# A decoder block on one core: three column blocks of w_in side by side over the chunks of x, and later side work

## The chip, the cores and the metric

The kernel runs as one program on 1 core of one Trainium2 chip. The engines are TensorE (PE, with PEld for the loading of its stationary operand), VectorE (DVE), ScalarE (ACT), GpSimd (POOL) and SyncE (SP). The metric is the device time of one execution in microseconds (us). Before the change it is 1447.08 us, the median of three runs (1445.6 to 1448.22).

## The reference

One block of a decoder for 256 tokens of width 2048, all in float32:

```python
h = rmsnorm(x, ln_mix_g)
u_s5, q, f, i, g, gate_s5, gate_hgrn = split(h @ w_in)           # w_in: 2048 x 9216
y_s5   = s5_branch(u_s5, ...) @ w_proj_s5        # diagonal complex scan over time, then a GLU
y_hgrn = hgrn2_branch(q, f, i, g, ...) @ w_proj_hgrn             # gated linear recurrence, 8 heads
x = x + (sigmoid(gate_s5) * y_s5 + sigmoid(gate_hgrn) * y_hgrn) @ w_out
x = x + conv_glu_ffn(rmsnorm(x, ln_ffn_g), w_up, conv_w, conv_b, w_down)   # d_ff = 5632
return rmsnorm(x, ln_final_g)
```

The S5 branch has 64 groups of 16 channels with 64 complex states each. The change touches how the first product, `h @ w_in`, begins, and when the S5 branch is computed beside it.

## The kernel before

**Weights as a stream of steps.** Every large product is cut into jobs of 256 or 512 columns, and each job into steps of one weight tile of [128, 1024] (512 KB). There are 480 steps, run in the order of the list `steps`; the first 144 are w_in, the next 8 the GLU of S5, then 16 of `w_proj_s5`, then `w_proj_hgrn` from step 168 on. For each step SP loads the tile (`load_step`, L247, four buffers `wr`), ACT casts its high part `wh` (L256) and DVE subtracts the low part `wl` (`split_step`, L252, three buffers of each), and PE forms three products: high by high, high by low, low by high. A feature-major job (`fm_job`, L271; u, q, f and the GLU) has 24 matmuls of 256 columns in a step, a token-major job (`tm_job`, L304) 12 of 512. Loads are issued 5 steps ahead (`LOAD_AHEAD`), splits 2 steps ahead (`LA`).

**x.** x comes in four chunks of 512 columns, two DMAs each (`load_x_chunk`, L388). `x_chunk` (L393) transposes a chunk on PE with the identity from the constant array `cf`, and ACT and DVE write its high and low parts to `hT`, with the gain `ln_mix_g` on columns (`g_mix`). The rows' norms come in after the products: `x_norm` (L427) squares x in eight DVE instructions, takes a root on ACT and a Newton step on DVE, and broadcasts the result over the partitions with matmuls of diagonal tiles `dg` into `R_x` (L358). `x_params` (L440) transposes the packed parameters to `colA`.

**The front's order before.** Jobs run one after the other, so step g of the first job needs chunk g of x. SP issues `cf`, `ln_mix_g`, then chunk and weight tile in turn. Chunks 1 to 3 are transposed in the middle of steps 0 to 2 (`st.between`, L284 and L1327), and `x_norm` and `x_params` are emitted behind step 2 (`NORM_AT`). A product's epilogue is emitted one step after its job's last step (`run_later`, L1274).

**Who sets the order.** The program's text gives priorities; the framework's scheduler then fixes, when the program is built, the order of each engine's queue, from its own model of times, and may move an instruction ahead of one that it takes to be waiting. On the chip each engine runs its queue strictly in that order. `issue_after` (in `behind_x`, L414) keeps an instruction behind a given one.

**Side work.** S5 (`side_s5`, L570) and then HGRN2 (`side_hgrn`, L866) are generators that are advanced between weight steps (`side_run`, L1290). Two counters add up estimated costs of DVE and PE (`_dve_cost`, `_pe_cost`, L76 and L84); a piece of side work is emitted as long as DVE's counter is not above PE's, at most two pieces of S5 or three of HGRN2 in a step, from step `S5_START` = 3 on. DVE's counter is never left more than 4 us behind. The GLU's steps need all of S5, and step 168 all of HGRN2: what is missing by then is emitted at once (`force`).

S5 works through eight chunks `ct` of 128 channels. For each, `tables` (L730) adds angles on POOL (L734), rounds them on ACT (L737) and takes sines; `b_place` and `b_trans` (L746, L756) transpose the input matrices, and POOL copies 24 blocks of 32 rows to other partitions (`move`, L754); `b_proj` (L771) multiplies them into the PSUM bank `bu`; DVE rotates, scans and rotates back; `output` (L782) multiplies the states into `ax`, and after chunks 3 and 7 a GELU and a split give the GLU's operand `z`. The four matrices of S5 are loaded from ACT's queue at its beginning (L574 to L577).

PSUM holds two `mm` banks for products, one `bu`, and two `ax` for transposes and small products.

Of the kernel before, what the change touches and what calls it, by code (L numbers as in the profile page):

```python
# [30 lines left out]
# columns of the constant array  # L31
# [5 lines left out]
def _constants():  # L37
# [12 lines left out]
    # within blocks of 32: per level, the columns in second halves of blocks of 2L; then the diagonal  # L50
# [6 lines left out]
# 1/(2 pi) in parts of twelve bits  # L57
# [37 lines left out]
class Metered:  # L95
    """An engine that adds up what its instructions are estimated to take."""
# [14 lines left out]
def kernel(  # L111
# [29 lines left out]
    NORM_AT = 2  # L141
# [25 lines left out]
    class Chunks:  # L167
        """[128, n, 256] kept in units of four."""
# [17 lines left out]
    S.dma_start(out=cf, in_=cst_f)  # L186
# [11 lines left out]
    S.dma_start(out=packG, in_=rows(ln_mix_g))  # L198
# [41 lines left out]
    def weight_step(src, mm, need=None, extra_load=None):  # L240
        st = Step()
        st.src, st.mm, st.need, st.extra_load = src, mm, need, extra_load
        st.after = st.between = None
# [60 lines left out]
    def tm_job(wap, c0, width, nkc, kper, xs, epi, need=None, extra_load=None, apart=False):  # L304
        """psum[t, n] for the columns from c0 on; xs(kc) gives the stationary pair."""
# [4 lines left out]
        for g in range(ng):  # L310
            def mm(st, g=g):
# [10 lines left out]
                # all of a row's products together in a last round of several tiles, else the low parts last  # L322
# [22 lines left out]
    def rstd_of(dst, ssum, n, scale, bias=None):  # L345
        """dst = 1/sqrt(ssum*scale + eps) for [128, n]; a Newton step after the square root."""
# [11 lines left out]
    def broadcast_rows(dst, r):  # L358
        """dst[p, j*128 + t] = r[t, j] on every partition."""
# [18 lines left out]
    def warm_up(n, rhs):  # L378
        # matmuls that nothing reads keep the tensor engine's clock up until the first products
# [3 lines left out]
    def table_up():  # L383
        # the square root's table comes in before x does
# [8 lines left out]
    def x_chunk(g, between=None):  # L393
        """Four chunks of x*g, transposed and in two parts; the rows' norms come in after the products."""
        for h in range(2):
            if h == 1 and between is not None:
                between()
# [5 lines left out]
            for a in range(2):  # L403
                kc = 4 * g + 2 * h + a
                A.activation(out=hT[:, kc, 0, :], in_=ax[:, a * T:(a + 1) * T], func=AF.Copy, scale=g_mix[:, kc:kc + 1])
# [5 lines left out]
        box["x"] = [getattr(i, "ins", i) for i in (last, lastp)]  # L411

    @contextmanager
    def behind_x():  # L414
        """What is emitted here is queued behind the last chunk of x."""
        with tc.issue_after(box["x"][0]), tc.issue_after(box["x"][1]):
            yield

    def x_first():
# [3 lines left out]
        x_chunk(0, lambda: split_step(steps[0]))  # L423
        with behind_x():
            warm_up(WARM_H, ones)

    def x_norm():  # L427
        ss = cst.tile([P, 2, 4], F32, name="ss_x")
        for g in range(4):
# [961 lines left out]
```

## Time and profile before

| | |
|---|---|
| median of 3 runs | 1447.08 us (1445.6 to 1448.22) |
| the profiled execution's own time (its span) | 1446.9 us |
| busy: PE, PEld | 1408.5 us (97%), 1209.1 us (84%) |
| busy: DVE, ACT, POOL | 1065.1 us (74%), 749.1 us (52%), 205.6 us (14%) |
| mean granted TensorE clock | 0.989 |
| HBM read, written | 266.73 MB, 10.49 MB |

A timeline row gives start, duration, engine, line, operation, output<-inputs and count; in brackets stands the idle time of that engine before it and what ended it. L106 is the helper through which all PE and DVE instructions are recorded, so these are told apart by their tiles. A row of the waits gives who waited for whom, the total in us, the number of waits and the longest. A row of a stretch gives the busy time of PE, PEld, DVE, ACT and POOL, with the number of instructions in brackets, then the granted clock, the DMA share and GB/s. Busy time of PE is that of overlapping, pipelined matmuls; idle time of PE is what can be gained.

### The profile page before, as it was taken

To read this page: it belongs to the slowest core of one execution; us is meant where nothing else is said; L and a number is where in the kernel's file an instruction comes from. 1 tells how busy PE (TensorE), PEld (TensorE's weight loads), DVE (VectorE), ACT (ScalarE), POOL (GpSimd) and SP (SyncE) were. 2 spreads that over 40 slices of the span, in tenths; PEclk is the share of its full clock that TensorE was granted. 3 is DMA by queue.
4 is the path that set the end of the run, shared out by engine and by line. 5 is a ranking of instruction groups with operands and counts; after the bars stand their busy time and mean duration, and the time that the engine had idled before them with its cause. 6 is when DMAs were issued, how large, how long until landed. Compare 5 with 4: busy or idle time off the path is not lost.

```text
span 1446.9 us, 21528 instructions
## 1 busy us (share of the span) xinstructions
PE 1408.5 (97%) x8328; PEld 1209.1 (84%) x8328; DVE 1065.1 (74%) x1435; ACT 749.1 (52%) x944; POOL 205.6 (14%) x230
## 2 busy tenths in 40 slices
PE   9997989899999999999999999999999999999997
PEld 8996887786778988888888888888888888888886
DVE  6978988999996967755677777777777775545454
ACT  5353466565554465445555555555555554434343
POOL 3037416743560100000000000000000000000000
PEclk9999999999999999999999999999999999999999
DMA  7763746565667656766666666666666665666563
GB/s 242 197 210 118 207 154 217 178 181 167 214 184 220 218 175 223 220 213 212 198 188 189 189 189 189 189 189 190 189 189 189 188 188 192 195 198 201 192 194 128
DMA packets 215942, 278.62 MB, mean 193 GB/s; under 512 B 19937, under 2 KB 141041, under 8 KB 215840
## 3 DMA queue, kind: packets, MB, share of 16 engines
q1 hardware_dynamic: 198496, 266.57, 59.6%
q10 hardware_dynamic: 17088, 10.49, 2.3%
q8 instruction: 65, 1.06, 0.3%
q14 instruction: 37, 0.30, 0.1%
q0 software_dynamic: 256, 0.19, 0.0%
HBM read 266.73 MB, written 10.49 MB: 192 GB/s over the span
## 4 chain that ended last, share of the span: by engine, by line
PE 82%; DVE 4%; POOL 3%; issue 1%; ACT 0%; DVEq 0%; ACTq 0%
PE mm L106 74%; PE ax L106 7%; POOL u L754 3%; DVE u L106 3%; DVE wl L106 1%; PE bu L106 0%; ACT wh L256 0%; POOL u L734 0%; ACT u L1262 0%; DVE zmat L106 0%; DVE x2g L106 0%; DVE t L106 0%; ACT t L260 0%; ACT t L1246 0%; DVE fin L106 0%
## 5 line engine op out<-in xcount | busy, mean ns | idle before, releaser
L106 DVE TENSOR_TENSOR wl<-wr,wh 128x1024 fp32r<-128x1024 f32 x480 | 596.4, 1246 | 323.8 <-ACT wh L256 321.6
L256 ACT CAST wh<-wr 128x1024 fp32r<-128x1024 f32 x480 | 502.8, 1051 | 607.3 <-PE mm L106 433.6
L106 PE MATMUL mm<-x2g,wh 128*128 128x512 f32 x1408 | 352.6, 392 | 0.0
L106 PEld LDWEIGHTS mm<-x2g,wh 128*128 128x128 f32 x1408 | 253.3, 189 | 45.3
L106 PE MATMUL mm<-wh,u 128*128 128x512 f32 x1040 | 259.7, 391 | 0.0
L106 PEld LDWEIGHTS mm<-wh,u 128*128 128x128 f32 x1040 | 194.1, 188 | 39.7
L106 PEld LDWEIGHTS mm<-x2g,wl 128*128 128x128 f32 x1408 | 192.0, 190 | 13.6
L106 PE MATMUL mm<-wh,hT 128*128 128x512 f32 x768 | 196.6, 399 | 4.9 <-ACT wh L256 4.9
L106 PE MATMUL mm<-x2g,wl 128*128 128x256 f32 x1408 | 196.4, 282 | 0.0
L754 POOL TENSOR_SCALAR u<-t 32x256 fp32r<-32x256 f32 x192 | 167.5, 874 | 163.1 <-ACT t L260 151.4
L106 PEld LDWEIGHTS mm<-wh,hT 128*128 128x128 f32 x768 | 145.5, 192 | 38.5 <-ACT wh L256 5.4
L106 PE MATMUL mm<-wl,u 128*128 128x512 f32 x520 | 140.6, 390 | 0.0
L106 DVE TENSOR_TENSOR u<-u,u 128x512 f32<-128x512 f32 (+3 forms) x134 | 114.0, 874 | 0.3
L106 PEld LDWEIGHTS mm<-wl,u 128*128 128x128 f32 x520 | 97.4, 188 | 19.9
L106 PE MATMUL mm<-wl,hT 128*128 128x512 f32 x384 | 106.0, 397 | 6.6 <-DVE wl L106 6.6
L106 PE MATMUL mm<-hT,wh 128*128 128x256 f32 x768 | 105.1, 289 | 4.4 <-ACT wh L256 4.4
L106 PEld LDWEIGHTS mm<-hT,wh 128*128 128x128 f32 x768 | 98.5, 196 | 5.6 <-ACT wh L256 4.6
L106 PEld LDWEIGHTS mm<-wl,hT 128*128 128x128 f32 x384 | 72.7, 191 | 24.9 <-DVE wl L106 9.5
L106 DVE SCALAR_TENSOR_TENSOR t<-ub,colC,t 128x256 f32<-128x256 f32 x176 | 73.3, 478 | 0.0
L106 PE MATMUL mm<-hT,wl 128*128 128x256 f32 x384 | 55.1, 286 | 0.0
L106 PEld LDWEIGHTS mm<-hT,wl 128*128 128x128 f32 x384 | 50.3, 195 | 0.2 <-DVE wl L106 0.2
L106 DVE TENSOR_TENSOR_SCAN u<-mag,u 128x256 f32<-128x256 f32 x64 | 47.9, 800 | 0.1
(191 smaller groups left out, 894.3 us busy)
## 6 DMA issues: line engine op xcount, KB each, us to landing
wr<-in_w_up_dram SPq DMA_DIRECT2D x176, 512.0 KB, 4.5
wr<-in_w_in_dram SPq DMA_DIRECT2D x144, 512.0 KB, 4.3
wr<-in_w_down_dram SPq DMA_DIRECT2D x88, 512.0 KB, 4.7
wr<-in_w_out_dram SPq DMA_DIRECT2D x32, 512.0 KB, 4.1
wr<-in_w_proj_s_dram SPq DMA_DIRECT2D x16, 512.0 KB, 4.1
wr<-in_w_proj_hgrn_dram SPq DMA_DIRECT2D x16, 512.0 KB, 4.9
d<-t ACTq DMA_DIRECT2D x28, 256.0 KB, 4.4
rl<-d SPq DMA_DIRECT2D x16, 256.0 KB, 3.8
```

Of the source, the lines that this page charges most:

```text
L106: return fn(*args, **kw)
L256: A.copy(st.wh, st.w)
L754: G.tensor_scalar(out=dst, in0=src.bitcast(F32), scalar1=1.0, scalar2=0.0, op0=ALU.mult, op1=ALU.add)
```

## The change

- The first three jobs of w_in run side by side (`FRONT = 3`): the first 12 steps are reordered, so that chunk g of x serves three steps. SP's loads follow: a chunk of x, then three weight tiles. The third job's sums lie in the bank `bu`.
- These 12 steps, and what goes with them, are in a fixed order on SP, PE, ACT and DVE (`manual_schedule`), with splits one step ahead. Chunks 1 to 3 are transposed ahead of steps 2, 5 and 8, not in the middle of a step.
- The squares of a chunk follow its transposition (`x_squares`), and the rest of the norm and `x_params` stand behind step 9 (`NORM_AT = 3 * FRONT`).
- `cf` and `ln_mix_g` are loaded from ACT's queue; the four parameter loads go behind w10 on SP, and HGRN2's masks behind the weight of step 12.
- The planner's counters begin at zero at step 12, and S5's side work begins there. `behind_x` also holds ACT's instructions.

The removed comments are left out of the diff.

```diff
-    NORM_AT = 2
+    FRONT = 3
+    NORM_AT = 3 * FRONT
...
-    S.dma_start(out=cf, in_=cst_f)
+    A.dma_start(out=cf, in_=cst_f)
...
-    S.dma_start(out=packG, in_=rows(ln_mix_g))
+    A.dma_start(out=packG, in_=rows(ln_mix_g))
...
-        S.dma_start(out=v3(st.w, st.src.shape[1]), in_=st.src)
+        st.dma = S.dma_start(out=v3(st.w, st.src.shape[1]), in_=st.src)
...
-    def fm_job(wap, c0, nkc, xs, epi, need=None, extra_load=None, wide=False):
+    def fm_job(wap, c0, nkc, xs, epi, need=None, extra_load=None, wide=False, bank=mm_bank):
...
-                    box["ps"] = mm_bank()
+                    box["ps"] = bank()
...
-                    if part == 1 and st.between is not None:
-                        st.between()
...
-    def x_chunk(g, between=None):
+    def x_chunk(g):
...
-        box["x"] = [getattr(i, "ins", i) for i in (last, lastp)]
+        box["x"] = [getattr(i, "ins", i) for i in (last, lastp, lasta)]
...
-        x_chunk(0, lambda: split_step(steps[0]))
-        with behind_x():
-            warm_up(WARM_H, ones)
+        x_chunk(0)
+        warm_up(WARM_H, ones)
+        split_step(steps[0])
+        x_squares(0)
+
+    ss_x = cst.tile([P, 2, 4], F32, name="ss_x")
+
+    def x_squares(g):
+        for j in range(2):
+            xc = x_tok[j][g // 2][:, (g % 2) * 512:(g % 2) * 512 + 512]
+            junk = tmp()
+            V.scalar_tensor_tensor(out=junk, in0=xc, scalar=1.0, in1=xc, op0=ALU.mult, op1=ALU.mult,
+                                   accum_out=ss_x[:, j, g:g + 1])
...
-    u_jobs = [fm_job(w_in, 256 * p, 16, xs_h, epi_u(p)) for p in range(4)]
+    def front_bank():
+        uid[0] += 1
+        return psb.tile([P, 2, 512], F32, tag="bu", name=f"mf{uid[0]}")
+
+
+    u_jobs = [fm_job(w_in, 256 * p, 16, xs_h, epi_u(p), bank=front_bank if p == 2 else mm_bank) for p in range(4)]
+    steps[:4 * FRONT] = [steps[4 * p + g] for g in range(4) for p in range(FRONT)]
...
-        S.dma_start(out=mraw[:, 0:112], in_=cst_m)
-        V.tensor_copy(masks, v3(mraw[:, 0:80], 5))
+        with behind_x(), tc.issue_after(getattr(steps[4 * FRONT].dma, "ins", steps[4 * FRONT].dma)):
+            S.dma_start(out=mraw[:, 0:112], in_=cst_m)
+            V.tensor_copy(masks, v3(mraw[:, 0:80], 5))
...
+    def load_front(i):
+        if i % FRONT == 0 and i < 4 * FRONT:
+            load_x_chunk(i // FRONT)
+        load_step(steps[i])
+        if i == 3 * FRONT + 1:
+            with tc.issue_after(getattr(steps[i].dma, "ins", steps[i].dma)):
+                load_params()
...
+    with tc.manual_schedule(engines={ET.SP, ET.PE, ET.Activation, ET.DVE}):
+        for i in range(LOAD_AHEAD):
+            load_front(i)
+        table_up()
+        warm_up(WARM, ones)
+        x_first()
+        for i in range(4 * FRONT):
+            g, r = divmod(i, FRONT)
+            load_front(i + LOAD_AHEAD)
+            if r == FRONT - 1 and g < 3:
+                x_chunk(g + 1)
+            split_step(steps[i + 1])
+            if r == FRONT - 1 and g < 3:
+                x_squares(g + 1)
+            work(i, steps[i])
+            if i == NORM_AT:
+                x_norm()
+                x_params()
+    for i in range(1, LA):
+        split_step(steps[4 * FRONT + i])
+    load["dve"] = load["pe"] = 0.0
+    for i, st in enumerate(steps):
+        if i < 4 * FRONT:
+            continue
...
-        if i >= S5_START:
-            pauses[0] = 0
-            if i == S5_START:
-                with behind_x():
-                    side_run()
-            else:
+        pauses[0] = 0
+        if i == 4 * FRONT:
+            with behind_x():
                 side_run()
+        else:
+            side_run()
```

`work(i, st)` is the old loop's body from `run_later(i=i)` to the entry of the epilogue, without the norm.

More of the change, by code (lines that the diff above doesn't have):

```diff
@@ L242, in weight_step @@
         st.src, st.mm, st.need, st.extra_load = src, mm, need, extra_load
-        st.after = st.between = None
+        st.after = None
         steps.append(st)
@@ L391, in load_x_chunk @@
                         in_=x[0, j * P:(j + 1) * P, g * 512:(g + 1) * 512])
-    def x_chunk(g, between=None):
+    def x_chunk(g):
         for h in range(2):
-            if h == 1 and between is not None:
-                between()
             ax = axbank()
@@ L404, in x_chunk @@
                 kc = 4 * g + 2 * h + a
-                A.activation(out=hT[:, kc, 0, :], in_=ax[:, a * T:(a + 1) * T], func=AF.Copy, scale=g_mix[:, kc:kc + 1])
+                lasta = A.activation(out=hT[:, kc, 0, :], in_=ax[:, a * T:(a + 1) * T], func=AF.Copy,
+                                     scale=g_mix[:, kc:kc + 1])
             for a in range(2):
@@ L410, in x_chunk @@
                                               op0=ALU.mult, op1=ALU.subtract)
-        box["x"] = [getattr(i, "ins", i) for i in (last, lastp)]
+        box["x"] = [getattr(i, "ins", i) for i in (last, lastp, lasta)]
     @contextmanager
     def behind_x():
-        with tc.issue_after(box["x"][0]), tc.issue_after(box["x"][1]):
+        with tc.issue_after(box["x"][0]), tc.issue_after(box["x"][1]), tc.issue_after(box["x"][2]):
             yield
@@ L422, in x_first @@
         V.tensor_copy(g_mix, ax[:, 0:16])
-        x_chunk(0, lambda: split_step(steps[0]))
-        with behind_x():
-            warm_up(WARM_H, ones)
-    def x_norm():
-        ss = cst.tile([P, 2, 4], F32, name="ss_x")
-        for g in range(4):
-            for j in range(2):
-                xc = x_tok[j][g // 2][:, (g % 2) * 512:(g % 2) * 512 + 512]
-                junk = tmp()
-                V.scalar_tensor_tensor(out=junk, in0=xc, scalar=1.0, in1=xc, op0=ALU.mult, op1=ALU.mult,
-                                       accum_out=ss[:, j, g:g + 1])
+        x_chunk(0)
[9 more added lines that the diff above has]
+                                   accum_out=ss_x[:, j, g:g + 1])
+    def x_norm():
+        ss = ss_x
         ssum = cst.tile([P, 2], F32, name="ssum_x")
@@ L1284, in run_later @@
                 later.sort(key=lambda e: (e[0], e[1]))
-    S5_START = 3
     PAUSES = {"s5": 2, "hgrn": 3}
@@ L1313, in side_run, with work @@
                     return
-    for i in range(LOAD_AHEAD):
-        if i < 4:
-            load_x_chunk(i)
+    def load_front(i):
+        if i % FRONT == 0 and i < 4 * FRONT:
+            load_x_chunk(i // FRONT)
         load_step(steps[i])
-        if i == 4:
-            load_params()
-    table_up()
-    warm_up(WARM, ones)
-    x_first()
-    for i in range(1, LA):
-        split_step(steps[i])
-    for i in range(3):
-        steps[i].between = lambda i=i: x_chunk(i + 1)
-    load["dve"] = load["pe"] = 0.0
-    for i, st in enumerate(steps):
-        if i + LOAD_AHEAD < len(steps):
-            load_step(steps[i + LOAD_AHEAD])
-        if i + LA < len(steps):
-            split_step(steps[i + LA])
+        if i == 3 * FRONT + 1:
+            with tc.issue_after(getattr(steps[i].dma, "ins", steps[i].dma)):
+                load_params()
+    def work(i, st):
         run_later(i=i)
@@ L1344 @@
         st.mm(st)
-        if i == NORM_AT:
-            with behind_x():
-                x_norm()
-                x_params()
         if st.after is not None:
@@ L1351 @@
             later.append((i + 1, job, fn))
-        load["dve"] = max(load["dve"], load["pe"] - 4.0)
-        if i >= S5_START:
-            pauses[0] = 0
-            if i == S5_START:
-                with behind_x():
-                    side_run()
-            else:
+    ET = mybir.EngineType
+    with tc.manual_schedule(engines={ET.SP, ET.PE, ET.Activation, ET.DVE}):
[22 more added lines that the diff above has]
+            continue
+        if i + LOAD_AHEAD < len(steps):
+            load_front(i + LOAD_AHEAD)
+        if i + LA < len(steps):
+            split_step(steps[i + LA])
+        work(i, st)
+        load["dve"] = max(load["dve"], load["pe"] - 4.0)
+        pauses[0] = 0
+        if i == 4 * FRONT:
+            with behind_x():
                 side_run()
+        else:
+            side_run()
     run_later(i=len(steps) + 10)
```

## The prediction

> **What bounds the kernel now.** I read the page first, then stretches of 20 us, the waits of the tensor engine, and the timeline of the first 50 us and of the places where it waits. Columns of a timeline row: start, duration, engine, line, operation, out<-in, count, and in brackets the idle time before it with what ended it.
>
> ```profile
> span 1446.9 us, 21528 instructions
> PE 1408.5 (97%) x8328; PEld 1209.1 (84%) x8328; DVE 1065.1 (74%) x1435; ACT 749.1 (52%) x944; POOL 205.6 (14%) x230
> ...
> 120.00:140.00 20.00, 13.75 (x59) 9.99 (x57) 19.06 (x19) 3.56 (x4) 17.26 (x21) 1.00 0.36 105
> ...
> PE mm L106 <- ACT wh L256: 9.3, 2, 4.9
> ```
>
> PE is busy for 1408.5 of 1446.9 us, so 38 us at most is there to win, and most of it is not in the front: the worst stretch is 120 to 140 us, where PE has 13.75 us of work while DVE has 19.06 and POOL 17.26. The two waits for `wh` (9.3 us together, the longer 4.9) belong to S5's side work. No matmul is added or dropped by the change, so I cost waits and starts, against this execution's 1446.9 us. The median of the runs, 1447.08, is 0.2 above it.
>
> **The change part by part.** First the front, with the rows from which each step has its duration:
>
> ```profile
> 0.74 0.38 SPq L186 DMA_DIRECT2D cf<-in_cst_f_dram  x1
> 1.65 0.88 SPq L390 DMA_DIRECT2D u<-in_x_dram  x2
> 5.71 0.33 PE L106 MATMUL ax<-cf,u 128*128 128x128 f32 x1 [1.19 <-DMA u<-in_x_dram]
> 8.79 1.06 ACT L256 CAST wh<-wr 128x1024 fp32r<-128x1024 f32 x1
> 9.91 2.73 PE L106 MATMUL mm<-hT,wh 128*128 128x256 f32 x16
> 20.56 0.81 PE L106 MATMUL ax<-cf,u 128*128 128x128 f32 x6
> 20.97 1.57 ACT L405 ACTIVATE hT<-ax,g_mix 128x256 fp32r<-128x256 f32 x4 [0.73 <-PE ax L106]
> 21.84 1.66 DVE L106 SCALAR_TENSOR_TENSOR hT<-ax,g_mix,hT 128x256 fp32r<-128x256 f32 x4 [0.16 <-ACT hT L405]
> 23.42 0.68 DVE L106 SCALAR_TENSOR_TENSOR t<-u 128x512 f32<-128x512 f32 x1
> 29.45 0.15 DVE L106 TENSOR_REDUCE ssum_x<-ss_x 128x2 f32<-128x8 f32 x1
> 29.52 1.22 DVE L106 TENSOR_TENSOR wl<-wr,wh 128x1024 fp32r<-128x1024 f32 x1
> 29.64 0.29 ACT L350 ACTIVATE rss<-ssum_x,epsd 128x2 f32<-128x2 f32 x1 [1.36 <-DVE ssum_x L106]
> 33.13 0.16 DVE L106 TENSOR_TENSOR rss<-rss,rsv 128x2 f32<-128x2 f32 x1
> 33.72 0.48 DVE L106 TENSOR_SCALAR dg<-cf,r_x 128x128 f32<-128x128 f32 x2
> 37.47 0.27 PE L106 MATMUL ax<-cf,u 64*128 64x64 f32 x1 [1.30 <-DVE R_x L106]
> 47.10 1.12 PE L106 MATMUL mm<-hT,wl 128*128 128x256 f32 x8
> 48.06 2.08 PE L106 MATMUL mm<-hT,wh 128*128 128x256 f32 x16
> 49.98 1.12 PE L106 MATMUL mm<-hT,wl 128*128 128x256 f32 x8
> ...
> 461.09 1.07 PE L106 MATMUL mm<-wl,hT 128*128 128x512 f32 x4
> 463.81 1.07 PE L106 MATMUL mm<-wl,hT 128*128 128x512 f32 x4
> ```
>
> (a) *Constants to the second queue.* `cf` and `ln_mix_g` stand before x on SP, so x is issued at 1.65; in the new kernel x has SP's place at 0.74. The first x reaches PE at 5.71 after a wait for its DMA, and from there transposes, four evictions on ACT and the first CAST (8.79) lead to the first product at 9.91. All of it moves up by 1.65 − 0.74: **−0.9 us**. Bounds −0.9 and 0. ACT now issues the two small loads, 0.4 us each, ahead of its table load, and idles until its first eviction at 7.35 anyway.
>
> (b) *Squares spread.* The eight squares stand in one block on DVE, from 23.4 us to the split (1.22) ahead of the reduction at 29.45, so to 28.2, 0.6 apart. Splits of weights queue behind them, their buffers come free late, loads and CASTs slip, and the copy of `R_x` stands behind a late `wl`. PE, whose transpose at 37.47 needs that bank, waits 1.3 us. Spread over the chunks, this goes: **−1.3 us** (bounds −1.3 and 0).
>
> (c) *Norm in fixed order.* But the broadcast of the norm now stands on PE's queue right behind step 9, and step 10 behind it. Count from the end of the last chunk's transposes, which precede step 8. In the old rows these end at 21.37 (20.56 + 0.81), ACT's evictions start at −0.40 and end at +1.17, DVE's low parts end at +2.13 (21.84 + 1.66 − 21.37). In the new order ACT then casts `wh9` (1.06, to 2.1), DVE subtracts `wl9` (1.22, to 3.4), does two squares (to 4.6), `wl10` (to 5.8), and the reduction. Behind that, uncrowded, come ACT's root (0.19 later, 0.29 long) and six small DVE operations, 0.15 to 0.2 apart (four lie from 33.13 to 33.72), with the last one's 0.28: about 1.9 us from reduction to broadcast, so 7.6. PE has only steps 8 and 9 in between, each 2.88 (49.98 − 47.10): it runs dry at 5.8. **+1.8 us**, bounds 0 (if the squares are done earlier) and 3.5 (with the clock, below). Behind the waiting broadcast stand step 10 and all later products; DVE's `R_x` and `colA` copies, `wl11` and the first epilogue follow within 3 us, and `wl11` is wanted 5 us later, so nothing else is late.
>
> The half clock has its own rows (window, busy times of PE, PEld, DVE, ACT, POOL, granted clock, DMA):
>
> ```profile
> 4.33:7.74 3.41, 1.81 (x13) 1.34 (x13) 0.46 (x2) 0.39 (x2) 3.29 (x9) 1.00 1.00 314
> 7.74:11.16 3.42, 3.42 (x19) 3.33 (x18) 2.93 (x5) 2.11 (x5) 3.42 (x4) 0.50 1.06 389
> ```
>
> A stretch in which PE had 1.81 us of work in 3.41 was followed by one at clock 0.50. A wait of 1.8 us leaves 1.6 if it falls into one such stretch, which for an unknown phase is (3.41 − 1.8)/3.41 = 0.47 likely; its price is at most 3.41/2 = 1.7 us. I take 0. The Trainium skill (TensorE: Matmul & The Clock Gate, "What's actually happening") says that the clock drops after a whole idle window of about 3.4 us; by that there would be no such loss, while the row above shows a drop after a window that was half busy, so the bound stays.
>
> (d) *Other loads and the order of products.* Twelve steps take 12 × 2.88 us in either order; the 24 transposes (0.135 each) only stand before the products instead of among them. SP issues w1 and w2 before the second chunk of x, and x's third and fourth chunks behind loads that wait for a buffer; each chunk is wanted three steps (8.6 us) after the last, and even the first x, with the queue cold, was there 4.1 us after its issue (1.65 to 5.71), so nothing waits. The four parameter loads (0.4 us of SP each) go behind w10 and the mask load behind w12; their readers come at step 9 and in HGRN2. The third job's bank is S5's, first needed 20 steps later. All nothing. But S5's four matrix loads now follow step 12 on ACT's queue:
>
> ```profile
> 35.27 4.38 ACTq L575 DMA_DIRECT2D u<-in_s_b_im_dram  x1
> ...
> 43.93 2.95 ACT L256 CAST wh<-wr 128x1024 fp32r<-128x1024 f32 x3 [8.11 <-DVE u L106]
> ```
>
> For 8.1 us, to 43.93, ACT casts nothing and issues. Three split weights ahead are 3 × 2.88 = 8.6 us of cover, against 8.1 us of it and a CAST of 1.06: **+0.6 us** (bounds 0, as before, and 1.5).
>
> (e) *S5's loop of eight chunks.* Emission of side work follows a planner: per step PE gains 24 × 0.109 = 2.616 and DVE 0.065 + 0.00112 × 1.04 × 1024 = 1.258, and side work fills the 1.358 between. Adding up the code's own cost functions, S5 is 193.4 of DVE and 19.0 of PE. Before, DVE's lead from the squares lets it begin at step 6; now the counters begin at step 12 with zero. Replaying the two counters, `b_trans` of chunks 0, 1, 2 comes at steps 27, 29, 44 before and 33, 35, 49 after; the tables of chunks 1 and 2 at 37 and 50 before, 42 and 57 after. What hangs on that distance:
>
> ```profile
> 99.64 36.62 POOL L754 TENSOR_SCALAR u<-t 32x256 fp32r<-32x256 f32 x48 [22.38 <-ACT t L260]
> 136.35 2.17 POOL L734 TENSOR_TENSOR u<-u 128x1024 f32<-128x1024 f32 x1
> ...
> 138.55 1.15 ACT L737 ACTIVATE u<-u,roundc 128x1024 f32<-128x1024 f32 x1 [14.24 <-POOL u L734]
> 140.69 3.65 PE L106 MATMUL mm<-wh,hT 128*128 128x512 f32 x8 [4.92 <-ACT wh L256]
> ...
> 162.17 19.93 POOL L754 TENSOR_SCALAR u<-t 32x256 fp32r<-32x256 f32 x24 [23.66 <-ACT t L260]
> 182.18 3.80 POOL L734 TENSOR_TENSOR u<-u 128x1024 f32<-128x1024 f32 x2
> ...
> 186.27 3.78 PE L106 MATMUL mm<-hT,wh 128*128 128x256 f32 x16 [4.39 <-ACT wh L256]
> ```
>
> POOL copies 48 blocks (36.6 us), then adds the table; ACT's rounding waits for it at the head of its queue, the CASTs wait behind it, and PE runs out of weights. For chunk 1 the distance shrinks from 10 steps to 9, and four of them become steps of 2.72 us (463.81 − 461.09): PE runs dry 2.88 + 4 × 0.16 = 3.5 us earlier, and one more half-clock stretch (1.7) follows: +5.2. For chunk 2 it grows from 6 steps to 8, which covers the 4.39 us and the half clock behind it (16 products in 3.78 us there against 2.08 at full clock, and 0.9 more on the rest): −7.0. Sum **−1.8 us**, bounds −7.0 and +5.2. For chunks 3 to 7 I count no difference.
>
> (f) *S5's end.* By the same counters S5 ended at step 140; now it would end at 145, and step 144, the first of the GLU, forces the rest out just before it. Its chain:
>
> ```profile
> 464.81 1.07 PE L106 MATMUL ax<-u,u 128*32 128x256 f32 x16
> ...
> 466.75 1.06 ACT L797 ACTIVATE u<-u 128x1024 f32<-128x1024 f32 x1 [0.38 <-DVE u L106]
> ...
> 468.98 1.05 ACT L260 CAST u<-u 128x1024 fp32r<-128x1024 f32 x1
> ...
> 470.25 1.22 DVE L106 TENSOR_TENSOR u<-u,u 128x1024 fp32r<-128x1024 f32 x1
> ```
>
> From the end of the output products (465.88) to the low part (471.47) are 5.6 us, which five steps hid. Now step 144 alone (first half of z, 2.88) lies over them; a weight's CAST in the middle (0.9) can go behind: 5.6 − 2.9 − 0.8 = **+1.9 us**, bounds 0 and 5.
>
> (g) *HGRN2* is emitted at steps 145 to 166 instead of 141 to 161, and step 168 needs it. It ran to 557.04 (row below), two steps behind its emission; now it would end as step 168 starts: **+0.5 us**, bounds 0 and 4.
>
> ```profile
> 556.58 0.46 ACT L1031 ACTIVATE u<-ax,colA 128x256 fp32r<-128x256 f32 x1
> ```
>
> Sum: −0.9 − 1.3 + 1.8 + 0.6 − 1.8 + 1.9 + 0.5 = +0.8; 1446.9 + 0.8 + 0.2 = **1447.9 us**. The front gives back its gain, and S5's shift gives and takes.
>
> **Rivals.** *The first POOL wait does not grow* (the scheduler puts the rounding behind one more CAST, or the table's addition ahead of the copies, as no table after chunk 2's made PE wait for `wh`: two such waits in all). Then 1447.9 − 5.2 = 1442.7. Against it: both early tables did make it wait.
>
> *Short distances come back* (the other side). In the replay chunks 5, 6 and 7 have six steps between `b_trans` and the next table, where they had seven; the one distance of six before is chunk 2's, and it cost 7.0. It decides if POOL's 24 copies outlast those six steps, 6 × 2.72 = 16.3 us, and ACT already stands at the rounding; chunk 2's took 19.93. Once is 1447.9 + 7.0 = 1454.9. For it: the copies are slower where DVE is full. The Trainium skill (SBUF — State Buffer, "Who interferes with whom") says that GpSimd's reads are blocked for a whole DVE instruction with two SBUF inputs; 36.62/48 = 0.76 and 19.93/24 = 0.83 us a copy here agree with a length that varies. Against it: chunks 3 to 7 made no CAST wait.
>
> *The side work is late at both ends*: (f) and (g) at their bounds, 1447.9 + 3.1 + 3.5 = 1454.5, if DVE too is behind at step 144. Against it: that last stretch had DVE idle.
>
> *The change does not shorten the front at all*: x's landing unmoved, (a) = 0, with (c) as costed: 1448.8, inside the forecast's band; so is (c) hidden, 1446.1.
>
> **How the numbers follow.** A measurement of this kernel tells about 0.2%, 2.9 us, from no change, so "same" is 1444.2 to 1450.0. Forecast 0.36; first wait does not grow 0.33 (faster); short distances 0.21 and late side work 0.10 (slower, 0.31). The likeliest case's own range is 1444 to 1450. For 8 in 10: down to 1440.5 (the faster case and another 2.2, (a) to (d) at their better ends), up to 1456 (the slower cases and 1.1 more).
>
> **What would show it.** (a) x's first issue at 0.7 and the first product near 9.0. (b), (c): no wait for `R_x`, but a wait of PE for `dg` of 1 to 2.5 us at 41 to 45 us. (d) A wait for `wh` under 1.5 us near 60 us. (e) One wait for `wh` of 7 to 9 us near 150 us, and none near 190. (f) A wait for `u` before step 145, near 482 us. It is wrong if the loop's waits of PE for `wh`, `wl` and `bu` differ in sum by over 5 us, or if the front ends over 2 us earlier than before.

## The result, and the profile after

The changed kernel takes **1459.53 us** (median of 4 runs, 1457.74 to 1460.66) against 1446.86 us before (4 runs, 1445.6 to 1448.22): ratio **1.0081**, 95% interval 1.0066 to 1.0095. It is slower by 12.7 us; the forecast was 1447.9, the range ended at 1456.0. The profiled execution is the quickest of the four: 1457.74 us for a span of 1455.7, so some 2 us of a time lie outside the span. The spans differ by 8.8 us.

The page after, its span and busy times:

```profile
span 1455.7 us, 21517 instructions
...
PE 1404.8 (97%) x8328; PEld 1204.1 (83%) x8328; DVE 1062.3 (73%) x1435; ACT 750.2 (52%) x946; POOL 193.2 (13%) x230
```

PE is busy for 3.7 us less than before, and still the span is longer: what was added is waiting. PE's waits after (who waited for whom: us in total, times, longest):

```profile
PE mm L106 <- ACT wh L257: 16.1, 6, 7.7
PE bu L106 <- POOL u L762: 13.5, 6, 6.5
PE mm L106 <- DVE wl L106: 6.1, 5, 2.7
PE ax L106 <- DVE dg L106: 2.1, 2, 1.9
PE ax L106 <- DMA u<-in_ln_mix_g_dram: 1.4, 1, 1.4
```

The wait for `R_x` is gone. Waits for `wh` grew from 9.3 to 16.1 us, and those of `bu` for POOL's copies from 7.0 (longest 2.5) to 13.5 (longest 6.5). To place the loss I took from both timelines the end of every step's low-part products (`mm<-…wl`) and subtracted:

| steps | terms of the prediction | foreseen, us | difference gained in the trace, us | sum so far |
|---|---|---|---|---|
| 0 to 11 | (a), (b), (c) | −0.4 | −1.3 | −1.3 |
| 12 to 15 | (d) | +0.6 | +1.9 | +0.7 |
| 16 to 63 | (e), chunks 1 and 2 | −1.8 | −2.1 | −1.4 |
| 64 to 143 | (e), chunks 3 to 7 | 0 | **+7.0** | +5.6 |
| 144 to 175 | (f), (g) | +2.4 | +3.2 | +8.8 |

From step 175 to the end the difference stays at 8.8 us. So most of the loss is where the prediction counted "no difference". Its own sign of being wrong is there too: PE's waits for `wh`, `wl` and `bu` add up to 35.7 us, against 24.6 before, and a difference of 5 was its limit. First the front, in the timeline after:

```profile
5.69 1.35 PE L106 MATMUL ax<-cf,u 16*128 16x16 f32 x9 [1.44 <-DMA u<-in_ln_mix_g_dram]
...
9.19 2.05 PE L106 MATMUL mm<-hT,wh 128*128 128x256 f32 x15 [0.81 <-ACT wh L257]
...
43.26 0.68 PE L106 MATMUL ax<-dg,ones 128*128 128x128 f32 x4 [1.94 <-DVE dg L106]
...
52.65 0.72 PE L106 MATMUL ax<-cf,u 64*128 64x64 f32 x4
...
59.05 2.94 ACT L257 CAST wh<-wr 128x1024 fp32r<-128x1024 f32 x3 [9.09 <-PE mm L106]
60.15 2.18 PE L106 MATMUL mm<-hT,wh 128*128 128x256 f32 x16 [1.00 <-ACT wh L257]
```

The first product starts 0.7 us earlier than the old 9.91 and runs at full clock (15 matmuls in 2.05 us, where 16 took 2.73). Its start differs from one execution to the next, though: among the kernels of this study it lies at 9.11 to 10.07 us in the nine with the new front and its two queues, at 9.91 to 11.34 in the four with the old front. The norm makes PE wait 1.94 us, and ACT casts nothing for 9.09 us while it issues S5's matrices.

Now chunk 3 and the table of chunk 4, before (PE's rows and POOL's and ACT's of one timeline, in order of engine):

```profile
214.76 24.66 POOL L754 TENSOR_SCALAR u<-t 32x256 fp32r<-32x256 f32 x24 [28.78 <-ACT t L260]
239.50 2.79 POOL L734 TENSOR_TENSOR u<-u 128x1024 f32<-128x1024 f32 x1
...
229.70 2.08 PE L106 MATMUL mm<-wl,hT 128*128 128x512 f32 x4 [2.10 <-DVE wl L106]
...
235.02 0.63 PE L106 MATMUL bu<-u,u 128*128 128x256 f32 x4
...
259.32 1.14 ACT L737 ACTIVATE u<-u,roundc 128x1024 f32<-128x1024 f32 x1
```

and after:

```profile
234.26 25.85 POOL L762 TENSOR_SCALAR u<-t 32x256 fp32r<-32x256 f32 x24 [28.18 <-ACT t L261]
...
246.70 0.51 PE L106 MATMUL bu<-u,u 128*128 128x256 f32 x2 [1.55 <-POOL u L762]
253.74 0.80 PE L106 MATMUL bu<-u,u 128*128 128x256 f32 x2 [6.53 <-POOL u L762]
254.33 3.06 PE L106 MATMUL mm<-wh,hT 128*128 128x512 f32 x8
...
282.56 17.12 POOL L762 TENSOR_SCALAR u<-t 32x256 fp32r<-32x256 f32 x24 [22.44 <-ACT t L261]
299.75 3.80 POOL L742 TENSOR_TENSOR u<-u 128x1024 f32<-128x1024 f32 x2
...
301.71 1.15 ACT L745 ACTIVATE u<-u,roundc 128x1024 f32<-128x1024 f32 x1 [13.87 <-POOL u L742]
...
303.84 3.78 PE L106 MATMUL mm<-wh,hT 128*128 128x512 f32 x8 [7.66 <-ACT wh L257]
```

Two queues fail here. **The products of a chunk stand too close behind its copies.** Before, 20.3 us lay between the first copy and the first `bu` product (214.76 to 235.02), with a wait of PE of its own in it (2.10), and the product found its blocks ready. After, PE comes to it 10.9 us behind the first copy (246.70 − 1.55 − 234.26), and waits 1.55 and then 6.53 us. **A table's addition stands behind one more chunk of copies.** Before, the addition whose result ACT rounds at 259.32 ran at 239.50, behind chunk 3's copies, 17 us ahead of its reader. After, no addition follows chunk 3's copies: it comes behind chunk 4's, at 299.75, in one row with the next. ACT stands at the rounding for 13.87 us, the CASTs stand behind it, and PE runs dry for 7.66 us. Each wait is followed by slow products: 8 of 512 columns in 3.06 and 3.78 us, which take 1.98 at full clock. Step 71 so took 13.2 us and step 85 13.0, where a step without side work takes 2.7.

Of chunk 3's 24 copies, one stands out. The second alone runs from 235.61 to 243.10, and in that stretch POOL executes nothing else, while DVE has no pause (busy us and instructions of PE, PEld, DVE, ACT and POOL; clock, DMA share, GB/s):

```profile
235.61:243.10 7.49, 7.49 (x35) 6.20 (x34) 7.49 (x11) 4.88 (x5) 7.49 (x1) 1.00 0.69 220
```

The shortest copies take 0.39 us, so this one is 7.1 us too long, nearly all of the 8.1 that PE waits here for chunk 3; no run takes it away by itself. The kernel before has such an event too, in chunk 4, a copy of 8.10 us:

```profile
262.45:270.55 8.10, 8.10 (x37) 6.70 (x37) 8.10 (x12) 3.94 (x4) 8.10 (x1) 1.00 0.81 253
...
278.35 0.50 PE L106 MATMUL bu<-u,u 128*128 128x256 f32 x2 [2.53 <-POOL u L754]
281.29 0.80 PE L106 MATMUL bu<-u,u 128*128 128x256 f32 x2 [2.43 <-POOL u L754]
```

Its step 80 took 10.1 us. The changed kernel has no long step there, so the +7.0 is a balance: two long steps against this one and some shorter ones.

### The profile page after: what moved, and what is told of

The parts are those of the page before. It is cut to its first block, busy times and chain, and to the rows that moved or that the text cites. A ratio compares the mean times of both kernels' runs of the same rounds, so it can differ in the third digit from the quotient of the medians.

```text
span 1455.7 us, 21517 instructions
## 1 busy us (share of the span) xinstructions
PE 1404.8 (97%) x8328; PEld 1204.1 (83%) x8328; DVE 1062.3 (73%) x1435; ACT 750.2 (52%) x946; POOL 193.2 (13%) x230
## 4 chain that ended last, share of the span: by engine, by line
PE 78%; POOL 5%; DVE 3%; ACT 2%; issue 1%; ACTq 0%; DVEq 0%
PE mm L106 71%; PE ax L106 6%; POOL u L762 5%; DVE u L106 1%; DVE wl L106 1%; PE bu L106 0%; ACT wh L257 0%; POOL u L742 0%; DVE t L106 0%; ACT t L479 0%; ACT t L1059 0%; ACT t L481 0%; ACT t L261 0%; ACT u L1271 0%; ACT L1059 0%
## 5 line engine op out<-in xcount | busy, mean ns | idle before, releaser
L762 POOL TENSOR_SCALAR u<-t 32x256 fp32r<-32x256 f32 x192 | 156.1, 814 | 182.8 <-ACT t L261 169.7
L106 PE MATMUL mm<-hT,wh 128*128 128x256 f32 x704 | 92.6, 284 | 4.3 <-ACT wh L257 4.3
L106 PEld LDWEIGHTS mm<-hT,wh 128*128 128x128 f32 x704 | 87.6, 192 | 5.6 <-ACT wh L257 5.1
L106 PE MATMUL mm<-hT,wl 128*128 128x256 f32 x352 | 49.5, 283 | 0.2 <-DVE wl L106 0.2
L1196 ACT ACTIVATE t<-ub,colC 128x256 f32<-128x256 f32 x88 | 48.0, 592 | 0.0
L106 PEld LDWEIGHTS mm<-hT,wl 128*128 128x128 f32 x352 | 45.4, 192 | 0.5 <-DVE wl L106 0.5
```

The lines of the kernel that those rows point to most:

```text
L106: return fn(*args, **kw)
L762: G.tensor_scalar(out=dst, in0=src.bitcast(F32), scalar1=1.0, scalar2=0.0, op0=ALU.mult, op1=ALU.add)
L1196: A.activation(out=av, in_=ub[:, a, 0:T], func=AF.Identity, scale=conv_col(0, n), bias=colC[:, 264 + n:265 + n])
```

## The experiments

My theory: S5's later place among the weight steps caused the loss, through POOL's copies and the two queues behind them; the rebuilt front by itself is worth little either way. The rivals: the front itself (its norm, its loads on other queues), or the amount of S5's delay as such (the later, the slower; or the end that step 144 forces). Ratios are against the kernel before on the same chip, with 95% intervals. All kernels compute the whole result.

**1. The old front, S5 from step 12 on.** The kernel before, with the place of S5 alone taken from the change:

```diff
-    S5_START = 3
+    S5_START = 12
...
     for i, st in enumerate(steps):
+        if i == S5_START:
+            load["dve"] = load["pe"] = 0.0
```

> The old front; S5's side work begins at step 12 with both counters at zero, so that it is emitted 5 to 7 steps later, as in the changed kernel. Theory 1 (the loss comes from where S5's loop now falls among the weight steps, not from the front): 1457 to 1461 us, 10 to 14 above the kernel before; in the trace PE's waits for wh, wl and bu sum to over 32 us, against 23 before. Rival (the new front itself, through the order the scheduler then makes of the rest, costs the time): within 3 us of the kernel before, 1444 to 1450.

Measured: 1458.12 us, ratio **1.0063** (1.0041 to 1.0085). Its waits:

```profile
PE mm L106 <- ACT wh L256: 15.9, 4, 7.7
PE bu L106 <- POOL u L754: 14.5, 7, 6.5
```

and in its timeline the rows that answer to those above:

```profile
252.94 0.80 PE L106 MATMUL bu<-u,u 128*128 128x256 f32 x2 [6.53 <-POOL u L754]
...
301.26 1.15 ACT L737 ACTIVATE u<-u,roundc 128x1024 f32<-128x1024 f32 x1 [13.89 <-POOL u L734]
```

The same two waits come in the same chunks, to 0.02 us, and the copy of 7.49 us is there too. From step 44 on its steps end 0.2 to 1.4 us ahead of the changed kernel's, and the waits for `wh`, `wl` and `bu` add up to 34.9 us, as the theory asked. The place of S5 alone makes the loss. It also ends step 11 at 49.6 us, the new front at 49.8: with S5 out of it the old front was as quick, in these two executions.

**2. The new front, S5 at its old place.** DVE's counter starts low and may stay low until step 40, so S5's pieces reach the old steps:

```diff
-    load["dve"] = load["pe"] = 0.0
+    load["dve"], load["pe"] = -7.0, 0.0
...
-        load["dve"] = max(load["dve"], load["pe"] - 4.0)
+        if i >= 40:
+            load["dve"] = max(load["dve"], load["pe"] - 4.0)
```

> The changed kernel, but the planner's counter of DVE begins at -7 at step 12 (and is not clamped before step 40): S5 catches up and, by a replay of the counters, stands from its first tables on at the same steps as before the change. Theory 1 (place of S5): the loss goes, 1444 to 1450 us, within 3 us of the kernel before. Rival (the new front through the later order): stays at 1457 to 1461.

Measured: 1454.79 us, ratio **1.0042** (1.0026 to 1.0059).

```profile
PE mm L106 <- ACT wh L257: 11.0, 3, 5.7
PE bu L106 <- POOL u L762: 8.1, 4, 5.3
```

Both expectations are missed: the theory's 1444 to 1450 us and the rival's 1457 to 1461. At step 39 it is 5.5 us behind the kernel before, and from there to the end the distance stays between 4.3 and 6.8, but for steps 79 to 98 (15.5 at step 79, then 7.7 to 8.2): nearly the same course through the chunks, the copy of chunk 4 that takes 8.1 us included. The 5.5 us arise before step 39. There S5's work of six steps is pressed into the first steps behind the front; that this is the reason is likely, and no run shows it. So this run does not show the old place without a loss; run 3 comes closest to that.

**3 and 7. Other places.** The same counter at −4.0 (S5 about three steps later than before) and at −1.4 (four to five later, a step earlier than in the changed kernel), without the `if`:

```diff
-    load["dve"] = load["pe"] = 0.0
+    load["dve"], load["pe"] = -4.0, 0.0
```

> The changed kernel with the planner's counter of DVE at -4 at step 12: S5 stands about three steps later than before the change, three earlier than in the changed kernel, and ends before step 144 without being forced. Theory 1a (the loss grows with the delay, because the end is pressed): about half of it, 1451 to 1455 us. Theory 1b (only how S5's pieces happen to fall counts, each chunk's wait for POOL appears or not): anywhere from 1444 to 1462, and in the trace the waits for POOL stand at other chunks. Rival (front): 1457 to 1461.

> The changed kernel with the planner's counter of DVE at -1.4 at step 12: by the replay S5's pieces stand 4 or 5 steps later than before the change, one step earlier than in the changed kernel; the end is still forced at step 144. Theory 1b (only how the pieces fall counts): the time differs from the changed kernel's ratio of 1.008 by over 3 us either way, with waits of 5 us or more at other chunks. Theory 1a (it grows with the delay): a ratio of 1.005 to 1.008.

Measured: three later 1449.47 us, ratio **1.0002** (0.9992 to 1.0011, 10 runs); five later 1455.69 us, **1.0045** (1.003 to 1.006).

Five later loses 10.7 us by step 70, has won them back at step 143 and ends 4.5 us behind: its long waits fall in other chunks than the changed kernel's. From the old place over three, four to five and six steps later the ratios run 1.0042, 1.0002, 1.0045 and 1.0081 (the changed kernel), 5 to 6 us from one to the next. From three steps on the time rises with the delay, so these totals alone do not rule out the delay as such. For the loop, run 8 below does: there S5 is no earlier than in the changed kernel, and at step 143 that run is 7.5 us ahead of the kernel before, where the changed kernel is 5.6 behind. Up to step 143 it is a matter of where each chunk falls. The end does go with the delay: from step 143 to 175 the old place loses 0.3 us, three steps later 1.7, four to five 4.3, six 3.2, and the kernels with S5 six steps late in runs 1, 4, 6 and 10 lose 3.1 to 3.8 too, with repairs or without.

**4 and 5. A third of the copies on ACT.** If POOL's copies are the first cause, shortening them must take away the loss *and* the sensitivity to the place. In both kernels, new and old:

```diff
-        def move(dst, src):
+        def move(dst, src, j):
+            if j == 2:
+                A.copy(dst, src.bitcast(F32))
+                return
             G.tensor_scalar(out=dst, in0=src.bitcast(F32), scalar1=1.0, scalar2=0.0, op0=ALU.mult, op1=ALU.add)
```

> The changed kernel, but one third of the block copies of S5 (the blocks that go to the third group of rows) are made by ACT instead of POOL: POOL's 24 copies of a chunk become 16, ACT gets 64 copies of about 0.4 us. Theory (POOL's copies are too long for the distance to the next table, and that is what PE waits for, as bu and through ACT's rounding as wh): the waits for bu fall from 13.5 us to under 5 and those for wh in the loop from 14 to under 5, and the time falls by 10 to 20 us, to 1440 to 1450. Rival (PE waits because DVE is full, POOL's lateness only takes the place of DVE's): waits for wl grow as the others fall, 1455 to 1461. Second rival (ACT's queue is the tight one): slower, over 1461.

> The kernel before (old front, old start of S5) with one third of S5's block copies made by ACT instead of POOL. Theory (POOL's copies set the distance to which PE's waits in S5's loop answer, so with shorter copies the place of S5 matters little): also below the kernel before, by 5 to 11 us (a ratio of 0.992 to 0.9965), and within 4 us of the changed kernel with the same copies on ACT, which was at 0.995; the 10 us between the two starts of S5 shrink to that. Rival (the place of S5 matters by itself, through DVE or the forced end): 8 to 12 us faster than that one, so a ratio of 0.987 to 0.990.

Measured: new front 1441.52 us, ratio **0.995** (0.9934 to 0.9967); old front 1439.3 us, **0.9938** (0.9923 to 0.9953). The new one's waits:

```profile
PE bu L106 <- DVE u L106: 4.7, 1, 4.7
PE mm L106 <- ACT wh L257: 3.8, 4, 1.4
```

and its group of copies on POOL (after the bar busy us and mean ns, then POOL's idle time before them):

```profile
L765 POOL TENSOR_SCALAR u<-t 32x256 fp32r<-32x256 f32 x128 | 118.1, 924 | 198.8 <-ACT t L261 190.9
```

No `bu` product waits for POOL any more, in either, though a single copy there is no shorter (924 ns, 814 in the changed kernel): there are 128 of them, not 192. A little of the first rival holds too: in the new front PE's waits for `wl` grew from 6.1 to 9.7 us, and one of 4.7 is for DVE. In the old front the waits for `wh` stayed (9.3 us before):

```profile
PE mm L106 <- ACT wh L256: 10.7, 8, 3.7
```

The longest comes behind a rounding on ACT that stands 9.38 us for POOL's addition: the second queue is still there. The two kernels, 12.7 us apart with all copies on POOL, are by their ratios 1.7 us apart, with intervals that overlap. Both beat the kernel before.

**6. The table's addition ahead of the copies.** In the changed kernel the addition for the next chunk goes to POOL before that chunk's copies; nothing else moves:

```diff
                 if ct < 7 and pair == 0:
+                    ahead = tables(ct + 1)
+                    next(ahead)
                     b_place(ct + 1)
...
-                    tab = yield from tables(ct + 1)
+                    tab = yield from ahead
```

> The changed kernel, but POOL adds up a chunk's angle table before it copies that chunk's blocks, not behind them; the work is the same. Theory (of PE's waits, those for wh come from ACT's rounding, which stands at the head of its queue until POOL has ended its copies): the waits for wh fall from 16 us to under 4 (the one of 1.0 behind S5's loads stays), those for bu stay at 10 to 15, and the time falls by 8 to 16 us with the half-clock stretches behind them, a ratio of 0.997 to 1.003 to the kernel before. Rival (PE would then wait for POOL's copies at the next bu instead, for as long): a ratio of 1.005 to 1.010 as the changed kernel, waits for bu over 20.

Measured: 1445.8 us, ratio **0.9981** (0.9972 to 0.9991, 10 runs): 14 us below the changed kernel.

```profile
PE bu L106 <- POOL u L762: 16.2, 6, 6.5
PE mm L106 <- ACT wh L257: 2.2, 3, 1.1
```

Waits for `wh` fall from 16.1 to 2.2 us while those for POOL's copies stay (13.5 before this edit, 16.2 now, a little over what I had put), the 6.53 us of chunk 3 among them. One at step 41 grew from 2.17 to 5.0 us: there the copies took over a part. The two queues are thus separate causes, and the waits for weights come through the table.

**8. The norm a step later.** In the changed kernel:

```diff
-    NORM_AT = 3 * FRONT
+    NORM_AT = 3 * FRONT + 1
...
-            later.append((i + 1, job, fn))
+            later.append((i + (2 if i < 4 * FRONT else 1), job, fn))
```

> The changed kernel with the norm and the parameters' transposition behind step 10 instead of step 9, and the first jobs' epilogues one step later. Theory of step (c) of the prediction (DVE's chain ends about 7.6 us after the last chunk's transposes, PE's two steps give 5.8 of cover): with a third step PE does not wait for dg, and the front ends 1.5 to 2.2 us earlier at step 12; the whole 0 to 3 us below the changed kernel (ratio to the kernel before 1.005 to 1.008). Rival (the chain is held up by PE or ACT itself and moves along): the wait for dg stays at 1.5 to 2.5 us.

Measured: 1450.66 us, ratio **1.0012** (1.0003 to 1.0022, 10 runs). The broadcast now waits 0.19 us:

```profile
44.41 0.68 PE L106 MATMUL ax<-dg,ones 128*128 128x128 f32 x4 [0.19 <-DVE dg L106]
```

and step 11 ends at 48.1 us, 1.7 earlier. The whole is 9 us below the changed kernel, far more than I had put (1.005 to 1.008) and than the norm can give. S5's pieces come at the same steps or one to two later, and both long waits are gone all the same: no copy of chunk 3 takes over 1.6 us, and the addition for chunk 4 runs on POOL ahead of chunk 4's copies (waits for `wh` 4.8 us). The next runs part the two.

**9 to 12. Both repairs together, and the small loads.** The copies' third on ACT and the early addition in the old front, in the new front, and in the new front with the norm a step later (edits of 4, 6 and 8); and the changed kernel with only this:

```diff
-    A.dma_start(out=cf, in_=cst_f)
+    S.dma_start(out=cf, in_=cst_f)
...
-    A.dma_start(out=packG, in_=rows(ln_mix_g))
+    S.dma_start(out=packG, in_=rows(ln_mix_g))
```

> The kernel before, with both repairs of S5's loop: the third column group of each block copy on ScalarE, and POOL's addition for the next chunk's tables ahead of that chunk's copies. All is computed. If the loss sits only in the two queues behind POOL's copies, the repairs add up: the third of the copies alone gave 0.9938 of the time before, and the table part is worth at most the waits for wh that it left (10.7 us), so 1429 to 1438 us, ratio 0.987 to 0.993, and PE's waits for wh fall below 4 us. If the table's place was worth something only where S5 came late, 1439 us as with the copies alone.

> The changed kernel with the same two repairs. All is computed. If the front's rearrangement is worth nothing by itself, as the run of the old front with S5 from step 12 on says, this and the old front with both repairs agree within 2 us (1430 to 1439 us). If the front is worth its first product 0.7 us earlier and its missing half clock, this one is 2 to 3 us faster. Waits for wh under 4 us, none of PE for POOL's copies over 2 us.

> The changed kernel with the two repairs, and the norm of x and the epilogues of the first three jobs a step later. All is computed. With the copies and the table out of the way the place of S5 matters little, so this shows what the norm is worth by itself: the wait for dg (1.9 us) goes, and the time is 1 to 2 us under that of the same kernel without it. If the earlier gain of 10 us with the norm a step later was the norm's own and not the loop's place, it is 8 to 10 us faster here too.

> The changed kernel, with the constants and the first layer's gain loaded on SP's queue ahead of x again; nothing else is changed and all is computed. If ScalarE's queue is what made the gain land at about 5.6 us, PE's transpose of it no longer waits for a load, x is issued some 0.9 us later, and the first product comes at 9.2 us or earlier, since x itself was no longer the last to arrive. If the second queue made no difference, the first product comes 0.9 us later, at 10.1. The time of the whole moves by 1 us from this, and by up to 5 us either way through where S5's loop falls, which tells nothing of the load.

| kernel | median, us | ratio, 95% interval |
|---|---|---|
| old front, both repairs | **1433.63** | **0.9895** (0.9867 to 0.9923) |
| new front, both repairs | 1436.14 | 0.9912 (0.9895 to 0.993) |
| new front, both repairs, norm a step later | 1436.31 | 0.9917 (0.9899 to 0.9934) |
| changed kernel, small loads on SP | 1461.73 | 1.009 (1.0072 to 1.0109) |

In both fronts the two repairs together beat one alone, as two queues ask, though they do not add up in full: in the new front they took 0.0131 (copies) and 0.0100 (addition) off the ratio one by one, and 0.0169 together. Shorter copies also bring the addition behind them earlier. The old front with both is the best version of the study, 15.5 us under the kernel before in the same runs (1449.15). Its waits for `wh` do not fall under the 4 us that I had put, nor do those of the new front (5.8):

```profile
PE mm L106 <- ACT wh L256: 5.3, 6, 1.8
```

No single one is over 1.8 us. Old and new front (2.5 us apart, where I had put 2) cannot be told apart there: the change, freed of its side effect, neither helps nor hurts by more than this measurement can tell. The norm a step later takes its wait away again (0.19 us), and yet the time is the same, so the norm's 1.9 us are real in the front and do not reach the end; they are given back in HGRN2's stretch: against the kernel before this one leads by 31 us at step 159 and by 11 at step 175, the one without it by 24 and 13. From step 151 to 175 PE idles for 4.4 us in it, 0.4 in the other. Why was not traced further. The 9 us of run 8 were not the norm's.

With the small loads on SP, PE in the front:

```profile
7.05 0.98 PE L106 MATMUL ax<-cf,u 128*128 128x128 f32 x7 [1.36 <-DMA u<-in_x_dram]
...
10.19 1.22 PE L106 MATMUL mm<-hT,wh 128*128 128x256 f32 x4
```

The gain no longer holds PE, but x does, and the first product comes 1.0 us later than in the profiled execution of the changed kernel, not earlier. What the queue does shows best in x itself: the second DMA of its first chunk lands at 5.87 to 6.14 us in the nine kernels with the small loads on ACT, at 6.72 to 7.32 in the five with them on SP. The first product shows it less surely: 10.19 lies just outside the 9.11 to 10.07 of those nine. At the end nothing of it can be told (1.009 against 1.0081).

## Why the prediction was wrong

**The step that failed is (e)**, in the words "For chunks 3 to 7 I count no difference". That stretch cost +7.0 us, of the 8.0 by which the profiled difference (+8.8) missed the sum (+0.8). What came in its place are waits of 1.55 and 6.53 us for chunk 3's copies, one of which took 7.49 us beside a DVE without pause, and one of 7.66 us for `wh` behind chunk 4's table. I took from the trace of before that these chunks had no wait for `wh` and let them stay so, though PE waited twice for POOL's copies in chunk 4 there (2.53 and 2.43 us), the change moved every chunk against the weight steps, POOL's copies (17 to 28 us a chunk from chunk 2 on) outlast five or six steps of 2.72 us, and the scheduler orders POOL's queue anew with each build. Runs 1, 3 and 7 show that the time depends on the place, runs 4 to 6 through which two queues. Having found an unknown phase in (c), I priced it there and not here.

**The rest of the miss**, 3.6 of 11.6 us, is in the reference point: a span was compared with the runs' times, and 0.2 us put between the two. After, they are 3.8 us apart: 2.0 lie outside the span, and the profiled execution is 1.8 below its median. Before, 1.7 to 1.9 us lie outside the span in every run that has both, so the profiled execution (1446.9) took about 1448.7, some 1.8 above its median. That is most of the difference between 8.8 us in the traces and 12.7 in the medians.

By term:

- (a) −0.9 foreseen; in the profiled pair the second DMA of x lands 0.7 us earlier (6.01, 6.72), and so comes the first product. The direction is right; the size of the gain at the first product lies within the spread from one execution to the next.
- (b) −1.3: the wait for `R_x` is gone, as foreseen, but the reason given is not shown. Runs 1, 5 and 9 have the old front with its block of squares and no such wait either; runs 5 and 9, with S5 early, have one of 1.0 and 0.9 us for `wh` at step 10 instead.
- (c) +1.8: a wait of 1.94 us for `dg` at 43.26. Right, in place and size. The half clock that I gave 0.47 and then left at 0 did not follow here, by luck: of the eight kernels with this wait it followed in four (runs 2, 4, 7 and 12), and steps 9 to 11 took 12.9 us in them, 11.4 in the other four.
- (d) +0.6: the wait for `wh` is 1.00. The stretch lost 1.9, since four transposes of S5 (0.7 us) that stood in the old front now stand behind step 12; I had not moved them along.
- (e), chunks 1 and 2: −1.8 foreseen, −2.1 measured, by luck: up to step 51 it was +2.1 (+5.2 foreseen), from there to step 63 −4.2 (−7.0 foreseen), two errors that cancel. The wait "of 7 to 9 us near 150" is 4.1 us, after 4.6 us of waits for POOL's copies in steps 37 to 41 that I had not put; and behind chunk 2's table PE still waits 1.04 and 1.42 us.
- (f) +1.9 and (g) +0.5: the sum, 2.4, came out at 3.2, its parts did not. (Term (f) takes off 0.8 us for a CAST that it gives as 0.9.) No product waited for `u` near 482; from step 143 to 151 the new kernel won 1.7 us, and it lost 4.8 from there to step 175. That is moved work and not waiting: 320 of HGRN2's small products went from the one stretch to the other, and PE idles there for 0.2 us. Of the 3.2, S5's last 16 output products (1.07 us, now behind step 143) and a wait of 0.77 us at 504.56 can be named; the rest stays open.

Of the rivals, *short distances come back* was on the right side with the right mechanism, POOL's copies that outlast the steps and are slower where DVE is full. Its size for one event was too small: 7.0 us, with the slow products, where steps 71 and 85 took 10.5 and 10.3 more than 2.7. It named chunks 5 to 7, by a replay of when pieces are emitted; it struck chunks 3 and 4, once as a wait for the copies themselves, which it did not speak of, and once because the addition had changed its place in POOL's queue, which the replay cannot see. At 0.21 it had too little of the chance, and the range too little room above: two such events, not one, were possible.

*The first POOL wait does not grow* came out as far as that wait goes (4.14 us, 4.92 before), but not in its reasons: the addition stood behind 48 copies again, and ACT at the rounding for 13.7 us.

*The change does not shorten the front* was half right: it does, by 1.3 us at step 11, but run 1 has the same from S5's start alone, and with the same front as here step 11 ended at 49.8 to 51.9 us (seven kernels), against 51.1 before.

## What to carry to other kernels

When side work is moved in time, every one of its pieces meets other work, also those that made no trouble before. A chunk without a certain wait in the old trace is no sign of slack, a wait of another kind beside it is a warning, and slow work that is handed on in strict queues (POOL's copies, then its addition, ACT's rounding, the CASTs, PE) must be costed by its length against the distance to its reader, for each piece, with a spread: here one copy of 0.4 us could take 8. It pays more to shorten the link that outlasts the distance, or to put what others wait for ahead of it in its queue, than to look for a better place: both repairs together gave 1.1% in the old front and made the place matter little. And a gain at the front counts only if nothing later absorbs it.

## What the runs showed of the hardware

**POOL's copies slow down beside DVE.** Two stretches of the changed kernel (busy us and instructions of PE, PEld, DVE, ACT, POOL; clock, DMA share, GB/s), both filled with the copies of chunk 3:

```profile
240.00:245.00 5.00, 5.00 (x23) 3.94 (x21) 5.00 (x7) 1.06 (x1) 4.88 (x4) 1.00 0.91 303
245.00:260.00 15.00, 6.92 (x26) 5.46 (x26) 9.91 (x11) 6.88 (x7) 13.73 (x20) 0.77 0.31 94
```

In the first, DVE is busy all the time, and POOL's four copies are the end of the one of 7.49 us (until 243.10) and three of 0.67 to 0.77. The second begins with five of 1.25 to 1.27 us and holds eleven of 0.40, all of them while DVE idles for 5.09 us (to 258.51). The Trainium skill (SBUF — State Buffer, "Who interferes with whom") has GpSimd's reads blocked during DVE's instructions with two inputs from SBUF; these rows agree. So do all 192 copies of this kernel: the 32 that had a tensor_tensor, scalar_tensor_tensor or scan beside them on DVE for less than a fifth of their length took 0.39 to 0.41 us, the 134 that had one for nearly all of it 0.92 on average, and the longest 7.49 (7.49 in runs 1, 6 and 12 too), with DVE going from one such instruction to the next. How much the DMAs moved does not order them (0.74, 0.76, 1.07 and 0.80 us on average beside under 100, 100 to 200, 200 to 300 and over 300 GB/s). The same copy on ACT (run 4) took 0.40 us on average. This also closes a loop: where PE waits and DVE runs dry, the copies speed up.

**A wait costs more than its length.** After 6.53 and 7.66 us of idle PE, 8 products took 3.06 and 3.78 us instead of 1.98, 1.1 and 1.8 us more. The granted clock stands at 0.50 for 6.83 us around each. The Trainium skill (TensorE: Matmul & The Clock Gate, "What's actually happening") lets the clock fall after a whole idle window of about 3.4 us; the second of these agrees (PE idle throughout from 297.57 to 300.98, 0.50 from there on). The first fell after a window in which PE had 0.51 us of work, and in run 7 it fell behind the wait of 1.94 us for `dg`, after one with 1.47:

```profile
41.10:44.51 3.41, 1.47 (x13) 1.29 (x12) 2.50 (x13) 2.18 (x3) 0.00 (x0) 1.00 0.80 263
44.51:47.92 3.41, 3.41 (x18) 3.41 (x18) 3.41 (x5) 0.00 (x0) 0.00 (x0) 0.50 0.15 47
```

So here the window need not be idle throughout, and a wait of 2 us can be enough.

**A small load on the second queue came late.** The gain (8 KB), issued on ACT's queue (kernel after: issue, KB, median us to landing), and before on SP's, in this order:

```profile
u<-in_ln_mix_g_dram ACTq DMA_DIRECT2D x1, 8.0 KB, 4.4
```

```profile
u<-in_ln_mix_g_dram SPq DMA_DIRECT2D x1, 8.0 KB, 1.8
```

Beside x on the other queue it took 2.6 us longer. With x itself landing at about the same time this cost PE little. Whether the cause lies in the queue or in x's packets was not tried.
